# Forming and storing inner Strassen weight sums earlier in a pooling-mixer layer

## The chip, the core and the metric

The kernel runs on one core of a Trainium2 chip. Its engines are named here as the profile names them: PE is TensorE (matrix products; PEld is its weight loads), DVE is VectorE, ACT is ScalarE, POOL is GpSimd and SP is SyncE, which here only issues transfers. GpSimd issues transfers too, on a queue of its own. The metric is the device time of one execution in microseconds; lower is better. "Faster" and "slower" compare the median of the changed kernel with that of the kernel before, run on the same chip.

## The reference

One layer of a pooling mixer on 4096 tokens of width 1024, all in float32, with a residual and a final RMS norm. `rms_norm` scales a row by the inverse root of its mean square and by a weight.

```python
def pool_mixer(h, in_w, group_w, group_b, scale, out_w):
    b, s, _ = h.shape
    u, gate = jnp.split(h @ in_w, 2, axis=-1)
    ug = u.reshape(b, s, POOL_GROUPS, POOL_GROUP_DIM)
    pooled = jnp.stack([trailing_mean(ug[:, :, g], w) for g, w in enumerate(POOL_WINDOWS)],
                       axis=2) - ug
    mixed = jnp.einsum('bsgc,gcd->bsgd', pooled, group_w) + group_b
    y = mixed.reshape(b, s, POOL_WIDTH) * scale * jax.nn.silu(gate)
    return y @ out_w

# out = rms_norm(x + pool_mixer(rms_norm(x, norm_w), ...), final_norm_w)
```

There are 4 channel groups of 256 with trailing windows of 2, 4, 8 and 16 tokens. The two large products are 4096 x 1024 times 1024 x 2048 and 4096 x 1024 times 1024 x 1024.

## The kernel before, in words

**Products.** Each float32 operand is split into a high part (a copy on ScalarE, rounded to the fast matmul type) and a low part (a subtraction on VectorE). A product of two such operands is three matmuls: high by high, high by low, low by high. Every block product is cut 2 x 2 and formed by the Strassen-Winograd scheme with seven products P1 to P7 instead of eight, over sums of the operands' quarters.

**Inner products.** Some of the seven are cut 2 x 2 once more. An input P7 then takes 84 matmuls of 256 columns (`product_seven`, L741 ff., matmuls at L753) where a plain one takes 48 of 512 (`mm3`, L807). In the output phase an inner P7 or P2 takes 42 of 256 (L949) where a plain one takes 24 of 512. Inner products need sums of the weight's quarters, each split in high and low part, and sums of the operand's quarters (`split_seven` for the input, `split_inner` for the output's P2).

**Steps.** The work is a row of steps, one for each of the seven products of a block. First come 28 steps "a": four blocks of 1024 tokens against the u half of the input weight, folded with the group maps. Then 28 steps "b": the same blocks against the gate half (gate blocks 0 to 3). Then the output phase, eight blocks "o" of 512 tokens. In a and b the order is P1, P2, P7, P6, P5, P4, P3, in o it is P1, P7, P6, P2, P5, P4, P3. P7 writes the PSUM banks that P1 and P2 filled, so it starts only when ScalarE has evicted them.

**What is inner before.** In the gate half P7 of blocks 1 and 2 (`inner_in`). In the output phase P2 from block 1 and P7 from block 2 (`OWN = 2`). The weight sums for the gate half's P7 are formed by `form_seven` in gate block 0, at P7, P6, P5 and P4, and stay on chip. Those of the output phase are formed in output blocks 0 and 1 (the table `forming`, with `load_inner`, `sum_inner`, `split_weight`).

**What sets the order.** A tile scheduler places the instructions on each engine, held by `issue_after` edges; from two steps ahead of output block `OWN` the order is the written one (`InOrder`, `steady`). Each engine works through its own row of instructions in order and stops at one whose inputs or whose tile's former users aren't done. The same holds for the two queues of transfers. Working tiles come from 11 `st` and 8 `vt` slots of 512 KB; operands in split form from four `op` tiles, two for each step. `take` hands out the slot that has been free longest, `keep` takes one for good, and a later load into a reused slot waits for all that read or wrote it. Nearly every copy, sum and transfer is recorded at L79, the line of a helper, so the tile names tell them apart: `op` are split operands, `w` split weights (`w_0_77`, `w_1_78` are the halves for P1), `bank` PSUM, `inner` a slot that holds an inner weight sum, `sd` the saved operands, `t3d`, `wod`, `wvd` weights in DRAM, `yd` the gated y in DRAM.

## Time and profile before

| | |
|---|---|
| median of 3 runs | 907.3 us (906.36 to 909.16) |
| profiled execution: device time | 907.23 us |
| profiled execution: span of the records | 905.4 us |
| TensorE busy | 895.8 us, 99% |
| VectorE, ScalarE, GpSimd busy | 84%, 57%, 13% |
| granted TensorE clock | 0.998 |
| an input step, plain (48 matmuls of 512) | 10.36 us |
| an input P7 with inner products (84 of 256) | 9.60 us |
| P1 of gate block 0 starts | 324.08 us |
| P7 of gate block 0 starts | 344.80 us |
| P7 of gate block 3 starts | 561.07 us |
| output block 0 starts | 612.98 us |
| period of an output block from block 2 on | 35.28 us |

The profile's times are microseconds from the span's start. A line of a timeline has the start, the duration, the engine, the line, the operation and the tiles (written from read), and in square brackets how long the engine was idle before it and what it waited for. "x12" is a group of 12. An engine's mean duration is longer than the distance of two instructions back to back, since they overlap by about 0.09 us. The granted clock is near full throughout. The span has a further few microseconds around it that the device time counts.

### The profile page before, as it was taken

How to read it: one execution, taken by the hardware profiler on the slowest of the kernel's cores; microseconds unless marked ns; L12 is line 12 of the kernel's file. 1: busy time of each engine (PE TensorE's matmuls, PEld its weight loads, DVE VectorE, ACT ScalarE, POOL GpSimd, SP SyncE). 2: the span in 40 equal slices, each digit the busy share in tenths (PEclk: the TensorE clock that was granted, in tenths of full speed). 3: DMA queues.
4: the chain of work that ended last, by engine and by line, in shares of the span. 5: the costliest groups of instructions: out<-in, count | busy, mean ns of one | idle time of the engine just before them, and what ended most of it. 6: DMA issues, size and time to landing. Idle time of an engine off the chain costs nothing.

```text
span 905.4 us, 12216 instructions
## 1 busy us (share of the span) xinstructions
PE 895.8 (99%) x4518; PEld 791.1 (87%) x4518; DVE 757.0 (84%) x925; ACT 517.5 (57%) x853; POOL 118.5 (13%) x208
## 2 busy tenths in 40 slices
PE   9999999999999999999999999999999999999996
PEld 7888888888888888889889888888889899999995
DVE  3899995985995999797599499599798878888797
ACT  7869547547445565346545636654657466565464
POOL 0020100100110000000000000001133333343330
PEclk9999999999999999999999999999999999999999
DMA  9987767577675453333554474638483865945953
GB/s 343 401 305 226 273 239 241 187 274 233 235 267 198 164 199 103 99 112 111 202 199 135 179 279 143 197 117 239 143 236 88 212 180 147 233 153 131 259 181 116
DMA packets 71692, 180.49 MB, mean 199 GB/s; under 512 B 6608, under 2 KB 24656, under 8 KB 71632
## 3 DMA queue, kind: packets, MB, share of 16 engines
q1 hardware_dynamic: 54976, 132.50, 42.6%
q0 software_dynamic: 15936, 46.16, 17.6%
q10 hardware_dynamic: 720, 1.06, 0.3%
q8 instruction: 35, 0.57, 0.3%
q14 instruction: 25, 0.20, 0.1%
HBM read 118.86 MB, written 60.83 MB: 198 GB/s over the span
## 4 chain that ended last, share of the span: by engine, by line
PE 87%; DVE 5%; ACT 3%; DMA 2%; issue 2%; POOL 0%; SPq 0%; DVEq 0%; ACTq 0%; POOLq 0%
PE bank L807 78%; PE bank L949 5%; DVE vt L79 2%; PE bank L753 2%; DVE op L79 2%; DMA st<-yd 1%; PE bank L447 1%; DVE st L79 1%; ACT op L79 1%; DMA early<-in_wut 1%; ACT st L79 1%; ACT w L79 0%; ACT vt L79 0%; DMA st<-wod 0%; DVE w L79 0%
## 5 line engine op out<-in xcount | busy, mean ns | idle before, releaser
L807 PE MATMUL bank<-op,w 128*128 128x512 f32 x2592 | 560.9, 379 | 0.1
L807 PEld LDWEIGHTS bank<-op,w 128*128 128x128 f32 x2592 | 489.4, 189 | 70.3 <-ACT vt L79 0.5
L807 PE MATMUL bank<-w,op 128*128 128x512 f32 (+1 forms) x1044 | 230.5, 377 | 0.0
L807 PEld LDWEIGHTS bank<-w,op 128*128 128x128 f32 x1044 | 192.3, 189 | 25.0
L79 DVE TENSOR_TENSOR op<-st,op 128x1024 fp32r<-128x1024 f32 x116 | 141.0, 1222 | 49.7 <-ACT op L79 49.3
L79 ACT ACTIVATE op<-st 128x1024 fp32r<-128x1024 f32 x116 | 121.4, 1051 | 68.7 <-PE bank L807 27.6
L79 ACT ACTIVATE op<-vt 128x1024 fp32r<-128x1024 f32 x67 | 70.4, 1053 | 59.3 <-DVE vt L79 38.7
L79 ACT ACTIVATE vt<-bank 128x512 f32<-128x512 f32 (+1 forms) x124 | 69.6, 580 | 48.0 <-PE bank L807 44.2
L79 DVE TENSOR_TENSOR op<-vt,op 128x1024 fp32r<-128x1024 f32 x67 | 80.9, 1221 | 17.5 <-ACT op L79 17.4
L79 DVE TENSOR_TENSOR st<-st,st 128x1024 f32<-128x1024 f32 (+1 forms) x55 | 63.9, 1181 | 17.6 <-ACT st L79 16.8
L79 POOL DMA_DIRECT2D vt<-in_x x26 | 23.3, 937 | 390.7 <-DVE vt L79 353.8
L79 ACT ACTIVATE bank<-bank 128x512 f32<-128x512 f32 (+1 forms) x78 | 38.7, 498 | 43.5 <-PE bank L807 32.1
L79 DVE TENSOR_TENSOR vt<-bank,vt 128x512 f32<-128x512 f32 (+1 forms) x94 | 54.2, 603 | 7.1 <-PE bank L949 4.6
L79 ACT ACTIVATE st<-bank 128x512 f32<-128x512 f32 (+1 forms) x58 | 33.0, 587 | 31.2 <-PE bank L807 17.4
L79 ACT ACTIVATE st<-st 128x1024 f32<-128x1024 f32 x33 | 34.8, 1056 | 22.6 <-DVE st L79 19.6
L79 DVE TENSOR_TENSOR st<-bank,st 128x512 f32<-128x512 f32 (+1 forms) x68 | 41.2, 625 | 7.4 <-PE bank L807 4.1
L79 DVE TENSOR_TENSOR st<-st,vt 128x1024 f32<-128x1024 f32 (+1 forms) x36 | 41.6, 1175 | 2.2 <-DMA vt<-rd 2.2
L949 PEld LDWEIGHTS bank<-w,op 128*128 128x128 f32 x312 | 40.4, 191 | 1.7
L949 PE MATMUL bank<-w,op 128*128 128x256 f32 x312 | 41.1, 275 | 0.0
L79 DVE TENSOR_TENSOR w<-st,w 128x1024 fp32r<-128x1024 f32 (+1 forms) x27 | 31.6, 1182 | 9.3 <-ACT w L79 9.2
L79 DVE TENSOR_TENSOR_SCAN vt<-vt,window 128x1040 f32<-128x1040 f32 x16 | 38.0, 2381 | 0.3 <-DMA yd<-vt 0.3
L79 DVE TENSOR_TENSOR vt<-vt 128x1024 f32<-128x1024 f32 (+3 forms) x42 | 37.6, 898 | 0.1
(115 smaller groups left out, 720.7 us busy)
## 6 DMA issues: line engine op xcount, KB each, us to landing
st<-in_xt SPq DMA_DIRECT2D x28, 512.0 KB, 6.2
sd<-st POOLq DMA_DIRECT2D x28, 512.0 KB, 4.4
st<-sd SPq DMA_DIRECT2D x26, 512.0 KB, 4.5
st<-in_x SPq DMA_DIRECT2D x21, 512.0 KB, 6.3
yd<-st SPq DMA_DIRECT2D x19, 512.0 KB, 2.9
vt<-yd SPq DMA_DIRECT2D x17, 512.0 KB, 10.4
out<-vt POOLq DMA_DIRECT2D x17, 512.0 KB, 3.3
st<-wod SPq DMA_DIRECT2D x16, 512.0 KB, 4.3
```

Source lines behind the costliest of these rows:

```text
L79: r = f(*args, **kwargs)
L447: latest[0] = nc.tensor.matmul(ps, a[:, kk, 2 * j + t, :], maps, start=t + m == 0, stop=t == 1 and m == len(pairs) - 1,).ins
L753: latest[0] = nc.tensor.matmul(cell(n, c).rearrange("p (a s) -> p a s", s=2), x1, x2, start=i == P1 and k + m == 0, stop=k == 1 and m == 2 ...
L807: latest[0] = nc.tensor.matmul(ps, a, b, start=start and n == 0, stop=stop and n == 2, skip_group_check=True).ins
L949: latest[0] = nc.tensor.matmul(ps, x1, x2, start=start and k + n == 0, stop=k == 1 and n == 2, skip_group_check=True,).ins
```

## The change

There are four parts.

1. P7 of gate block 0 gets inner products too (`inner_in`, and `split_reach` for its P6, lose the condition on the block). Its weight sums are formed in the last u block: the weight halves are loaded at its P7 (`load_seven`), summed at P6 (`sum_seven`), and split and stored to DRAM at P6 and P5 (`save_seven`, into `sevend`, on GpSimd's queue). At P2 of gate block 0 `take_seven` loads them back, into a quarter of P7's weight tiles and three kept slots.
2. P7 of the output phase is inner from block 1 (`OWN = 1`). The output phase's weight sums are formed in gate blocks 2 and 3: those of P2 at P4 and P3 of block 2 and P1 of block 3, those of P7 at P2, P7, P6 and P5 of block 3. `save_inner` stores them to `innerd`, and `take_inner` loads them in output block 0, again on GpSimd's queue.
3. With the sums gone from output blocks 0 and 1, the split of P2's operand outside the steady order (`split_inner`, `late_split`) and the gathering of slots (`gathered`, `split_weight`) go.
4. In the last output block the inner sums of P2 are added before the evictions instead of behind them, the split for P4 goes behind P2's product, and one row of the norm moves from P2 to P4.

GpSimd's queue has 24 rows more, VectorE 15, ScalarE 14, TensorE 9. The diff, cut to its core:

```diff
-OWN = 2
+OWN = 1
...
-        return q == 1 and 0 < b < NB - 1 and i == P7
+        return q == 1 and b < NB - 1 and i == P7
...
+    sevend = {p: dram.tile([P, 2, 2, 256], F32R, name=f"seven{p}") for p in (P4, P5, P6, P7)}
...
+    def save_seven(*ps):
+
+        for p in ps:
+            place = next_kept()
+            t = st.keep().rearrange("p v (k c) -> p v k c", k=2)
+            latest_copy[0] = copy(t[:, 0], seven["sums"][p]).ins
+            latest_split[0] = sub(t[:, 1], seven["sums"][p], t[:, 0].bitcast(F32)).ins
+            gpsimd.dma_start(out=sevend[p], in_=t)
+            give_kept(place)
...
+    def take_seven():
...
+        for p in (P6, P7, P4):
+            places_in.append(next_kept())
+            t = st.keep().rearrange("p v (k c) -> p v k c", k=2)
+            gpsimd.dma_start(out=t, in_=sevend[p])
+            seven_w[p] = [t[:, v] for v in range(2)]
+        seven_w[P5] = [w[P7][0][:, v, :, 0:256] for v in range(2)]
+        for v in range(2):
+            gpsimd.dma_start(out=seven_w[P5][v], in_=sevend[P5][:, v])
...
-    def split_weight(i, *ps):
+    def save_inner(i, *ps):
 
         for p in ps:
+            place = next_kept()
+            t = st.keep()
+            home = versions(t)
+            latest_copy[0] = copy(home[0], raws[i][p]).ins
+            latest_split[0] = sub(home[1], raws[i][p], home[0].bitcast(F32)).ins
+            gpsimd.dma_start(out=innerd[i][p], in_=t)
+            give_kept(place)
...
+    def take_inner(i, *ps):
+        for p in ps:
+            place = innerd[i][p]
             if p == P5:
-                home = [quarter(w[i][0][:, s], 1) for s in range(2)]
+                home = [quarter(w[i][0][:, v], 1) for v in range(2)]
+                for v in range(2):
+                    gpsimd.dma_start(out=home[v], in_=versions(place)[v])
             else:
-                t = kept.pop().rearrange("p k (h s a) -> p h k s a", h=2, s=2)
-                home = [t[:, s] for s in range(2)]
-            copy(home[0], raws[i][p])
-            sub(home[1], raws[i][p], home[0].bitcast(F32))
+                t = reserved.pop() if reserved else st.keep()
+                gpsimd.dma_start(out=t, in_=place)
+                home = versions(t)
             (own_w if i == P7 else inner_w)[p] = home
...
         if inner and i == P2:
             inner["rows"] = [hs[b][0, j][:, 0] for j in range(2)]
+            if final:
+                add_inner(0, (0, 0))
...
-        if inner and i == P2:
+        if inner and i == P2 and not final:
             add_inner(0, (0, 0))
...
-            split(ready[P4], s["22"])
-            give(s.pop("22"))
-            if final:
-                norm_row(b - 1, 0, 1)
+            if not final:
+                split(ready[P4], s["22"])
+                give(s.pop("22"))
...
             evict_o(b, P2, sets)
+            if final:
+                split(ready[P4], s["22"])
+                give(s.pop("22"))
...
-            if not final:
+            if final:
+                norm_row(b - 1, 0, 1)
+            else:
...
-        (0, P4): lambda: load_inner(P2),
-        (0, P3): lambda: sum_inner(P2),
-        (1, P1): lambda: split_weight(P2, P7, P6),
-        (1, P7): lambda: (split_weight(P2, P5, P4), end_weights(P2), load_inner(P7)),
-        (1, P6): lambda: sum_inner(P7),
-        (1, P5): lambda: split_weight(P7, P7, P6),
-        (1, P4): lambda: (split_weight(P7, P5, P3), keep_temps(P7)),
+        ("a", NB - 1, P7): load_seven,
+        ("a", NB - 1, P6): lambda: (sum_seven(), save_seven(P6)),
+        ("a", NB - 1, P5): lambda: (save_seven(P7, P4, P5), end_seven()),
+        ("b", 0, P2): take_seven,
+        ("b", NB - 2, P4): lambda: load_inner(P2),
+        ("b", NB - 2, P3): lambda: (sum_inner(P2), save_inner(P2, P7, P6)),
+        ("b", NB - 1, P1): lambda: (save_inner(P2, P4, P5), end_weights(P2)),
+        ("b", NB - 1, P2): lambda: load_inner(P7),
+        ("b", NB - 1, P7): lambda: sum_inner(P7),
+        ("b", NB - 1, P6): lambda: save_inner(P7, P7, P6),
+        ("b", NB - 1, P5): lambda: (save_inner(P7, P3, P5), end_weights(P7)),
+        ("o", 0, P6): lambda: take_inner(P7, P5),
+        ("o", 0, P2): lambda: take_inner(P7, P6, P7, P3),
+        ("o", 0, P5): lambda: take_inner(P2, P5),
+        ("o", 0, P4): lambda: (reserved.extend(st.keep() for _ in range(3)), keep_temps()),
+        ("o", 0, P3): lambda: take_inner(P2, P7, P6, P4),
```

On VectorE the first place is ahead of P7 of gate block 0. Before, the row with `op_85` is the low part of P7's first operand, and the two `w` rows are the low parts of P4's weights:

```order
L79 SCALAR_TENSOR_TENSOR st_95<-vt_107,colt,st_95 128x512 x2
L79 TENSOR_TENSOR op_85<-vt_101,op_85 128x1024
L79 MEMSET vt_106 128x2x16
L79 TENSOR_REDUCE window<-vt_106 128x1
L79 TENSOR_TENSOR w_0_674<-st_94,w_0_674 128x1024
L79 TENSOR_TENSOR w_1_675<-st_99,w_1_675 128x1024
L79 TENSOR_TENSOR op_86<-st_96,op_86 128x1024
L79 TENSOR_TENSOR vt_100<-st_90,vt_101 128x1024
L79 TENSOR_TENSOR vt_104<-st_98,st_96 128x1024
```

In the changed kernel, at the same place, where `op_85` is the low part of the front sums (the second inner operand of P7 that is read) and `op_86` that of the plain quarter read first:

```order
L79 TENSOR_TENSOR w_0_686<-st_2282,w_0_686 128x1024
L79 TENSOR_TENSOR vt_104<-st_92 128x512
L79 TENSOR_TENSOR w_1_687<-st_91,w_1_687 128x1024
L79 TENSOR_TENSOR vt_104<-vt_103,vt_104 128x512
L79 TENSOR_TENSOR op_86<-st_92,op_86 128x1024
L79 TENSOR_TENSOR vt_107<-vt_104,st_92 128x512
L79 TENSOR_TENSOR vt_107<-vt_103,vt_104 128x512
L79 TENSOR_TENSOR vt_102<-st_96,st_92 128x1024
L79 TENSOR_TENSOR st_91<-st_98,vt_103 128x1024
L79 TENSOR_TENSOR op_85<-vt_107,op_85 128x1024
```

The four sums of 512 (`vt_104`, `vt_107`) are new here, and the `w` rows and the form of P6's operand (`vt_102`, `st_91`) now come ahead of the operand's low part.

The second place is ahead of P7 of gate block 3. On SyncE's queue, before, the loads for P1's weights of the output phase (`wod1`) stand ahead of the stores of y:

```order
L79 DMA st3_92<-wod1_0_123 128x1024 [waits DMAHW3_49,DVE_49]
L79 DMA st7_3691<-wod1_1_124 128x1024 [waits DVE_49]
L79 DMA yd4_173<-st2_91 128x1024 [waits DVE_49,Activation_49]
L79 DMA yd4_173<-st4_93 128x1024 [waits DMAHW6_49,DVE_49,Activation_49]
L79 DMA yd5_174<-vt1_101 128x1024 [waits DMAHW7_49,DVE_49]
L79 DMA yd5_174<-vt2_102 128x1024 [waits DMAHW0_49,DVE_49]
L79 DMA st7_3691<-wod2_0_125 128x1024 [waits DMAHW4_49,DMAHW1_49,DVE_49]
```

In the changed kernel, where a DMASW in the list of waits is a transfer of GpSimd's queue (here the store of a saved sum):

```order
L79 DMA vt7_107<-wod2_1_126 128x1024 [waits DMAHW0_49,DVE_49]
L79 DMA st10_4083<-wod1_0_123 128x1024 [waits DMAHW3_49,DMAHW1_49,DMASW3_49]
L79 DMA yd5_174<-vt3_103 128x1024 [waits DVE_49]
L79 DMA yd5_174<-vt6_106 128x1024 [waits DVE_49]
L79 DMA st9_4088<-wod1_1_124 128x1024 [waits DMAHW4_49,DMAHW6_49,DMASW4_49,Activation_49]
L79 DMA st10_4083<-wod7_1_136 128x1024 [waits DMAHW5_49,DMAHW1_49,DVE_49]
L79 DMA st2_91<-wod2_0_125 128x1024 [waits DVE_49,Activation_49]
```

The first `wod1` load moved behind a saved sum's store, the second behind both stores of block 3's y and another saved sum's store. On ScalarE the copies of those weights stood well ahead of the evictions of P2's banks (`vt_103`, `st_92`), but for the first half of P2's weights (`w_0_79`):

```order
L79 ACTIVATE w_1_78<-st_3691 128x1024
L79 ACTIVATE op_87<-st_3690 128x1024
L79 ACTIVATE w_0_79<-st_3691 128x1024
L79 ACTIVATE vt_103<-bank_69 128x512
L79 ACTIVATE vt_103<-bank_70 128x512
L79 ACTIVATE st_92<-bank_71 128x512
L79 ACTIVATE w_1_80<-st_90 128x1024
L79 ACTIVATE st_92<-bank_72 128x512
```

and now:

```order
L79 ACTIVATE w_0_77<-st_4083 128x1024
L79 ACTIVATE op_86<-st_91 128x1024
L79 ACTIVATE vt_103<-tails 128x2x16
L79 ACTIVATE w_1_78<-st_4088 128x1024
L79 ACTIVATE vt_104<-bank_69 128x512
L79 ACTIVATE vt_104<-bank_70 128x512
L79 ACTIVATE w_0_79<-st_91 128x1024
L79 ACTIVATE st_96<-bank_71 128x512
L79 ACTIVATE w_1_80<-vt_107 128x1024
L79 ACTIVATE st_96<-bank_72 128x512
```

The copy of the second half of P1's weights (`w_1_78`, from the `wod1_1` load) now stands directly ahead of the first eviction, and that of `w_0_79` between the second and the third.

116 lines of the change are left out of this document (39 added, 77 removed).

## The prediction, as recorded before the run

> **What bounds the kernel now.** I read the page first, then the chain of waits, then the busy time of each engine step by step, and last single rows at the places that the change touches. From the page, the engines' busy time and the stores that GpSimd issues:
>
> ```profile
> PE 895.8 (99%) x4518; PEld 791.1 (87%) x4518; DVE 757.0 (84%) x925; ACT 517.5 (57%) x853; POOL 118.5 (13%) x208
> ...
> sd<-st POOLq DMA_DIRECT2D x28, 512.0 KB, 4.4
> ```
>
> TensorE is the bound over the whole span, so a gain must take matmul time away, and every microsecond that another engine delivers too late is paid in full. The chain of waits (start, length, what) shows what a step costs and the few places where TensorE waits:
>
> ```profile
> 417.48 9.60 PE bank L753 x84
> 427.08 62.16 PE bank L807 x288
> 489.24 9.60 PE bank L753 x84
> ...
> 555.99 3.40 DMA st<-wod
> 559.57 0.87 issue
> 560.44 0.59 ACT vt L79
> 561.07 80.57 PE bank L807 x372
> ...
> 671.19 0.94 PE bank L949 x6
> 672.13 2.59 PE bank L807 x12
> ...
> 689.64 1.34 PE bank L949 x12
> ```
>
> Six plain input steps take 62.16 us, 10.36 each; an input P7 with inner products (L753) takes 9.60. A plain matmul of 512 columns is 2.59/12 = 0.216 us, one of 256 columns 1.34/12 = 0.112. Three stalls stand in the second half. Six matmuls at L949 should take 0.67 us; at 671.19 they take 0.94 after a wait of 0.31, so 0.58 is lost. The last block has the same, worse: 0.61 + 0.27 = 0.88. The third is where P7 of gate block 3 waits for bank evictions until 561.07 (two steps' excess in the table below: 0.22 + 0.11 = 0.33).
>
> ```profile
> 671.19 0.94 PE L949 MATMUL bank<-inner,op 128*128 128x256 f32 x6 [0.31 <-DVE vt L79]
> ...
> 885.05 0.94 PE L949 MATMUL bank<-inner,op 128*128 128x256 f32 x6 [0.61 <-DVE vt L79]
> ```
>
> The busy times by step (window, length, then each engine's busy time) show how much room stands beside TensorE. The first three rows are P7, P6, P5 of the last u block, the next two its P4 and P3, then P1, P2, P7 of gate block 0; the last three are P1, P2, P7 of gate block 3:
>
> ```profile
> core 0: us, PE busy (x) PEld busy (x) DVE busy (x) ACT busy (x) POOL busy (x), PEclk, DMA share, GB/s
> 272.28:282.64 10.36, 10.36 (x50) 9.07 (x49) 5.96 (x6) 5.35 (x7) 0.00 (x0) 1.00 0.48 163
> 282.64:293.00 10.36, 10.36 (x50) 9.07 (x49) 6.29 (x8) 6.84 (x10) 0.00 (x0) 1.00 0.68 227
> 293.00:303.36 10.36, 10.36 (x50) 9.07 (x49) 7.82 (x11) 8.72 (x11) 0.00 (x0) 1.00 0.46 162
> 303.36:313.72 10.36, 10.36 (x50) 9.07 (x49) 10.36 (x12) 2.82 (x6) 0.00 (x0) 1.00 0.64 209
> 313.72:324.08 10.36, 10.36 (x50) 9.07 (x49) 10.36 (x13) 5.82 (x7) 0.00 (x0) 1.00 0.30 115
> 324.08:334.44 10.36, 10.36 (x50) 9.07 (x49) 10.36 (x12) 6.14 (x8) 0.00 (x0) 1.00 0.74 244
> 334.44:344.80 10.36, 10.36 (x50) 9.07 (x49) 10.33 (x14) 5.34 (x7) 0.00 (x0) 1.00 0.61 201
> 540.13:550.49 10.36, 10.36 (x50) 9.07 (x49) 10.29 (x10) 4.87 (x10) 0.00 (x0) 1.00 0.26 102
> 550.49:561.07 10.58, 10.52 (x49) 8.88 (x47) 10.52 (x12) 4.70 (x7) 0.00 (x0) 1.00 0.43 154
> 561.07:571.54 10.47, 10.47 (x49) 9.18 (x49) 9.99 (x9) 7.96 (x12) 0.00 (x0) 1.00 0.48 155
> ```
>
> VectorE has 4.40 + 4.07 + 2.54 = 11.0 us free before 303.36, and none from there to 344.80, nor from 540 to 561. The change puts VectorE work into or ahead of both full stretches. That decides this case.
>
> **Gains.** P7 of gate block 0 goes from 10.36 to 9.60: 0.76. P7 of output block 1 goes from 24 matmuls of 512 (5.18) to 42 of 256 (4.69): 0.49. In output blocks 0 and 1, sixteen VectorE rows that sum and split weights go away, and the steady order begins where VectorE is freer: I take the 0.58 as gone. Reading the inner sums first in the last block frees the first bank before the evictions: I take the 0.88 as gone too; the pieces moved behind (a split, a norm row) have the P5 to P3 products to hide under. Together 2.71. The earlier sums of output weights (gate blocks 2 and 3) cost TensorE nothing themselves; their price is at the second place below. The 24 new transfers on GpSimd's queue: 12 stores, 12 loads and the split loads; GpSimd is 13% busy and its loads for P7 of gate block 0 are issued where the front of the queue is free, so I cost their issue at nothing, and their landing below.
>
> **The first place: P7 of gate block 0.** Durations on VectorE, with spacing (back to back, a pair's length less one row's):
>
> ```profile
> 336.69 0.76 DVE L79 SCALAR_TENSOR_TENSOR st<-st,colt,st 128x512 f32<-128x512 f32 x1
> 337.36 1.42 DVE L79 SCALAR_TENSOR_TENSOR st<-vt,colt,st 128x512 f32<-128x512 f32 x2
> 338.68 1.23 DVE L79 TENSOR_TENSOR op<-vt,op 128x1024 fp32r<-128x1024 f32 x1
> ...
> 340.06 2.35 DVE L79 TENSOR_TENSOR w<-st,w 128x1024 fp32r<-128x1024 f32 x2
> ```
>
> So 1.13 for a row of 1024, 0.66 for a scaled row of 512; a plain row of 512 is 0.69 long (next fence), 0.60 spaced. Before, the operand of P7 is ready at 339.91, 4.9 us ahead of 344.80. Now ahead of it stand four weight sums, four low parts for the saves, four sums of the operand (4.8 + 2.4 us in rows of 512) and two rows of the P6 form and two of w4 (4.5 us, which stood behind): 11.7 us. The chain begins with loads that VectorE waits for at 291.90 and 295.85. SyncE's issues, then VectorE's rows, then the group of plain rows of 512:
>
> ```profile
> 286.85 0.38 SPq L79 DMA_DIRECT2D vt<-in_in_w  x1
> ...
> 290.42 0.34 SPq L79 DMA_DIRECT2D st<-t3d  x1
> ```
>
> ```profile
> 291.90 1.41 DVE L79 SCALAR_TENSOR_TENSOR vt<-vt,colt,st 128x512 f32<-128x512 f32 x2 [1.51 <-DMA vt<-in_in_w]
> ...
> 295.85 1.41 DVE L79 SCALAR_TENSOR_TENSOR st<-st,colt,st 128x512 f32<-128x512 f32 x2 [2.54 <-DMA st<-t3d]
> ```
>
> ```profile
> L79 DVE TENSOR_TENSOR inner<-vt,inner 128x512 fp32r<-128x512 f32 x4 | 2.7, 688 | 0.0
> ```
>
> Issue to use is 5.05 and 5.43. In the new order the load waits for two scaled rows fewer and is issued 1.3 us sooner, so the scaled rows start at 290.6. From there to the low part of the fourth saved sum stand 6 scaled rows, 5 of 1024 and 9 of 512: 4.0 + 5.7 + 5.4 = 15.1, ending at 305.7. Its store lands 4.4 later (310.1); only then may SyncE load the second t3 half into that slot, and 5.3 later (315.4) VectorE can scale with it. By its own work (6 more rows of 1024, 3 of 512: 8.6) it would be there at 314.3. Behind that load on SyncE stand the in_in_w loads for w4 and two y stores; none is wanted before VectorE has passed the scaling. From 315.4 to the low part of the front sums, P7's second inner operand, stand 14 scaled rows, 19 of 1024 and 6 of 512: 9.2 + 21.5 + 3.6 = 34.3, ending 349.7. TensorE wants it six short matmuls into the step, at 345.5: 4.2 late. ScalarE's three copies ahead of the inner moves (about 1.05 each) hold the next bank some 0.6 longer. So P7 is 4.8 late and 0.76 shorter: +4.0. Bounds: if VectorE comes to 303 with all the added rows done in its 11.0 us, nothing is late (-0.8); if landings are a third slower, as the busy DMA rows of 0.64 and 0.74 allow, 1.5 and 1.8 more (+7.3). I stay in the middle because the rows name each wait.
>
> [...]
>
> **The second place: P7 of gate block 3.** Here the weights w1 of the output phase must be copied by ScalarE before it may evict P2's banks, which P7 needs:
>
> ```profile
> 559.47 1.06 ACT L79 ACTIVATE w<-st 128x1024 fp32r<-128x1024 f32 x1 [5.88 <-DMA st<-wod]
> 560.44 1.07 ACT L79 ACTIVATE vt<-bank 128x512 f32<-128x512 f32 x2
> ...
> 552.59 0.32 SPq L79 DMA_DIRECT2D yd<-vt  x1
> 555.99 6.15 SPq L79 DMA_DIRECT2D st<-wod  x4
> ```
>
> Before, only the w2 copy stands ahead of the evictions, issued at 555.99 and used at 559.47 (3.48). Now the second w1 half does, and its load waits on SyncE behind both stores of y, and for the store of the last saved P2 sum to land. VectorE has eight rows of 512 more before the y rows (4.8 us): the last y store goes from 552.59 to 557.3, the last saved sum, 3.4 us of rows ahead, ends at 553.9, its store lands at 558.3, the load is issued then and used at 561.8. Copy (1.05) and eviction (0.6) end at 563.4 instead of 561.0: 2.6 late on a step that would start at 550.49 + 10.36 = 560.85. The third bank stands behind the w2 copy: its load follows a VectorE row four of 1024 behind the y rows (561.8), arrives 565.3, copy and eviction end at 566.9, where TensorE wants the bank at 563.4 + 2.6 = 566.0: 0.9 more. In all 3.5 in place of 0.33: +3.2. Bounds: nothing late (-0.3), or with landings as long as at the first place, twice 1.7 more (+6.6).
>
> **The sum.** The profiled run took 907.23 with a span of 905.4; the median of the runs is 907.3, so the sum is taken on 907.2. 907.2 + 4.0 + 3.2 - 0.49 - 0.58 - 0.88 = 912.5 us, 0.6% slower.
>
> **The rivals.** Other side: VectorE comes early. Its busy rows before 344 need not mean that it is behind: with 11.0 us idle before 303 it could run the moved rows there, and at gate block 3 likewise in the steps ahead of 518. It decides from 4.2 us earlier at the first place and 2.6 at the second. Against it: the sums hang on loads that land at 290.6 at the earliest. Then 907.2 - 0.76 - 0.33 - 1.95 = 904.2. Only the first place stalls: 907.2 + 4.0 - 0.33 - 1.95 = 908.9. Only the second: 907.2 - 0.76 + 3.2 - 1.95 = 907.7. Worse than forecast: a third place, where GpSimd's loads of the saved sums in output block 0 stand ahead of the x loads on its queue, and wait for VectorE's w3; a store and a load there (4.4) on top, 916.9. Against it: VectorE is freer there by sixteen rows. That the change would not do what it says is ruled out by the order of its instructions.
>
> **How the numbers follow.** Both places 0.56, VectorE early 0.16, only the first 0.09, only the second 0.06, worse 0.13. What a measurement can tell from no change is about 0.3%, 2.7 us: 904.6 to 910.0. Faster is the early case, 0.16. Same is the two single cases (0.15) and a tenth of the first, 0.21 in all. Slower is the rest, 0.63. The likeliest case alone spans 909.5 to 916. The range goes from 904.0, which takes in the early case, to 917.5, for the third place or the longer landings at one place.
>
> **What would show it.** In the new profile: the L753 group of 84 from about 345 ending near 359.2, with a wait for VectorE's op; a gap of about 2.6 before P7 of gate block 3 behind ScalarE's w1 copy from wod, and one of about 0.9 inside it; no wait of L949 for VectorE at the start of the steady order or in the last block. I am wrong if the operand's low part stands ready before 345.5, if ScalarE's w1 copy there ends by 560, or if TensorE waits at the first output blocks.

## The result and the profile after

The changed kernel takes 934.53 us (median of 5 runs, 933.53 to 935.35) against 907.3 us: the ratio is 1.0297, with a 95% interval from 1.0282 to 1.0313. The forecast was 912.5. The direction was right and the size was not: 27.2 us slower in place of 5.2. The profiled execution took 933.88 us with a span of 932.1. From the page, the engines' busy time:

```profile
PE 902.8 (97%) x4572; PEld 797.9 (86%) x4572; DVE 766.1 (82%) x939; ACT 523.1 (56%) x868; POOL 136.0 (15%) x235
```

TensorE has 54 matmuls more (the nine rows of the change are groups of six) and was "busy" 7 us longer, though the inner products should have taken 1.25 us of work away. A part of the time is therefore inside the matmuls, and the rest is waits. The loss of a step is the distance from its first matmul to that of the next step, less 10.36 us (9.60 for an inner P7 of the input). Laid out by place, in us:

| place | before | after |
|---|---|---|
| P6 and P5 of u block 2 | 0.10 | 0.77 |
| P1, P2, P7 of gate block 0 | none | 0.65, 3.78, 5.42 |
| P2 of gate block 1 | none | 1.21 |
| P2, P7 of gate block 3 | 0.23, 0.10 | 4.67, 1.91 |
| output block 1, whole period | 36.35 | 45.60 |
| from the last matmul to the end of the span | 7.0 | 8.1 |

Against the profile before, gate block 0 costs 9.85 of loss less the 0.76 that its inner P7 saves, +9.1; gate block 1 +1.2; gate block 3 +6.25; output block 1 +9.25; u block 2 +0.7 (the run with repeated low parts, below, changes nothing there and has 0.73 as well, so this isn't put down to the change); the tail +1.1. The stall in the last output block is gone, -0.9. The sum is +26.7, the difference of the spans. Three places carry it.

**The first place, P7 of gate block 0.** TensorE's timeline; the idle time before a group and what it waited for stand in the brackets:

```profile
349.89 0.94 PE L761 MATMUL bank<-op,w 128*128 128x256 f32 x6 [3.62 <-ACT vt L79]
351.69 0.58 PE L761 MATMUL bank<-op,w 128*128 128x256 f32 x1 [0.86 <-ACT op L79]
354.00 4.00 PE L761 MATMUL bank<-op,w 128*128 128x256 f32 x17 [1.74 <-DVE op L79]
```

The step begins with a wait of 3.62 us for an eviction on ScalarE, then waits for the high and the low part of its operand. And 17 matmuls of 256 columns take 4.00 us, 0.235 each, where 0.112 is usual. ScalarE's and VectorE's timelines show what was late:

```profile
307.32 0.63 ACT L79 ACTIVATE inner<-vt 128x512 fp32r<-128x512 f32 x1 [2.90 <-DMA seven<-inner]
...
348.30 1.06 ACT L79 ACTIVATE op<-vt 128x1024 fp32r<-128x1024 f32 x1 [2.48 <-DVE vt L79]
349.26 0.58 ACT L79 ACTIVATE vt<-bank 128x512 f32<-128x512 f32 x1
```

```profile
307.98 0.69 DVE L79 TENSOR_TENSOR inner<-vt,inner 128x512 fp32r<-128x512 f32 x1 [3.32 <-ACT inner L79]
...
319.38 1.41 DVE L79 SCALAR_TENSOR_TENSOR st<-st,colt,st 128x512 f32<-128x512 f32 x2 [2.09 <-issue]
...
347.51 0.69 DVE L79 TENSOR_TENSOR vt<-vt,vt 128x512 f32<-128x512 f32 x1
...
352.72 2.36 DVE L79 TENSOR_TENSOR op<-vt,op 128x1024 fp32r<-128x1024 f32 x2
```

ScalarE's copy of the front sums (348.30) waits for VectorE's second sum (347.51), and the eviction that P7's first matmul needs stands right behind that copy. VectorE works without a break from 319.38. Its first wait (307.98) is for ScalarE's copy of the fourth saved sum, which itself waited for the store of an earlier one to land (307.32). Its second wait is put down to "issue", but it ends 0.1 us behind the landing (319.29) of a load that SyncE issued at 312.41, 7.0 us before its use:

```profile
312.41 0.32 SPq L79 DMA_DIRECT2D st<-t3d  x1
```

**The second place, P7 of gate block 3.** From the chain of waits:

```profile
564.92 4.38 DMA inner<-inner
...
569.35 5.53 DMA st<-wod
...
574.92 0.94 issue
575.86 0.59 ACT vt L79
...
576.49 63.58 PE bank L815 x285
```

The store of a saved sum lands after 4.38 us, the load of `wod1_1` waits for it, lands 5.53 later, ScalarE copies it (0.94 to the next instruction), evicts, and TensorE starts.

**The third place, P7 of output block 1.** TensorE, then ScalarE's square root that holds up the move of the bank, then GpSimd's queue:

```profile
680.70 1.65 PE L957 MATMUL bank<-w,op 128*128 128x256 f32 x6 [7.56 <-ACT bank L79]
682.14 1.49 PE L957 MATMUL bank<-inner,op 128*128 128x256 f32 x6
683.42 2.67 PE L815 MATMUL bank<-w,op 128*128 128x512 f32 x6
```

```profile
676.41 0.29 ACT L79 ACTIVATE otmp<-oss,eps 128x2 f32<-128x2 f32 x1 [5.56 <-POOL oss L79]
```

```profile
645.24 0.91 POOL L79 DMA_DIRECT2D w<-inner  x1 [1.45 <-issue]
653.24 0.89 POOL L79 DMA_DIRECT2D w<-inner  x1 [7.08 <-issue]
...
666.84 0.91 POOL L79 DMA_DIRECT2D w<-inner  x1 [5.15 <-PE bank L815]
670.85 0.90 POOL L79 DMA_DIRECT2D w<-inner  x1 [3.10 <-issue]
...
676.15 0.23 POOL L79 TENSOR_TENSOR oss<-parts 128x2 f32<-128x2 f32 x1
```

GpSimd forms the sum of squares for the norm at 676.15. Ahead of it in its queue stand the loads of P5's saved sums (`w<-inner`, two for each sum, in pieces of 128 float32). The second of a pair is issued 8.0 and 4.0 us behind the first, and the wait before it has no releaser ("issue"). The second pair itself starts late, behind a wait of 5.15 us for TensorE.

### The profile page after: what moved, and what is told of

It reads as the page before. It is cut to its first block, busy times and chain, and to the rows that moved or that the text cites. A ratio compares the mean times of both kernels' runs of the same rounds, so it can differ in the third digit from the quotient of the medians.

```text
span 932.1 us, 12430 instructions
## 1 busy us (share of the span) xinstructions
PE 902.8 (97%) x4572; PEld 797.9 (86%) x4572; DVE 766.1 (82%) x939; ACT 523.1 (56%) x868; POOL 136.0 (15%) x235
## 4 chain that ended last, share of the span: by engine, by line
PE 43%; DVE 11%; issue 5%; DMA 5%; ACT 1%; POOL 1%; DVEq 0%; POOLq 0%; ACTq 0%; SPq 0%
PE bank L815 34%; PE bank L957 5%; DVE vt L79 5%; PE bank L761 3%; DVE st L79 3%; DVE op L79 2%; DMA vt<-yd 1%; DMA out<-vt 1%; ACT st L79 1%; DMA st<-wod 1%; DMA vt<-in_x 1%; DMA inner<-inner 0%; DVE w L79 0%; DMA st<-t3d 0%; DMA seven<-inner 0%
## 5 line engine op out<-in xcount | busy, mean ns | idle before, releaser
L815 PE MATMUL bank<-op,w 128*128 128x512 f32 x2544 | 553.2, 380 | 6.3 <-ACT vt L79 4.5
L815 PEld LDWEIGHTS bank<-op,w 128*128 128x128 f32 x2544 | 481.2, 189 | 76.8 <-ACT vt L79 4.9
L815 PE MATMUL bank<-w,op 128*128 128x512 f32 (+1 forms) x1020 | 227.2, 378 | 0.0
L79 DVE TENSOR_TENSOR op<-st,op 128x1024 fp32r<-128x1024 f32 x121 | 147.3, 1222 | 54.2 <-ACT op L79 53.8
L79 ACT ACTIVATE op<-st 128x1024 fp32r<-128x1024 f32 x121 | 126.9, 1052 | 73.5 <-PE bank L815 33.9
L957 PE MATMUL bank<-w,op 128*128 128x256 f32 x336 | 45.1, 278 | 7.6 <-ACT bank L79 7.6
L79 POOL DMA_DIRECT2D inner<-inner x14 | 7.7, 548 | 291.3 <-DVE inner L79 255.6
L79 ACT ACTIVATE st<-bank 128x512 f32<-128x512 f32 x56 | 32.2, 594 | 31.3 <-PE bank L815 19.1
L79 ACT ACTIVATE w<-st 128x1024 fp32r<-128x1024 f32 (+1 forms) x24 | 24.6, 1035 | 34.1 <-DMA st<-wod 21.5
L79 DVE TENSOR_TENSOR vt<-vt 128x256 f32<-128x256 f32 (+3 forms) x44 | 38.4, 876 | 0.1
```

Of the source, the lines that this page charges most:

```text
L79: r = f(*args, **kwargs)
L815: latest[0] = nc.tensor.matmul(ps, a, b, start=start and n == 0, stop=stop and n == 2, skip_group_check=True).ins
L957: latest[0] = nc.tensor.matmul(ps, x1, x2, start=start and k + n == 0, stop=k == 1 and n == 2, skip_group_check=True,).ins
```

## The experiments

All ratios are against the kernel before on the same chip, with their 95% intervals. The losses are read as in the table above, from the profiled execution, which isn't always near the median: it took 929.12 us in the first run on GpSimd's queue, 923.88 in the run without part 1 and 911.50 in the first of the two runs with a plain P7.

### The parts alone

The first run holds part 4 alone, in the kernel before (the diff of `norm_row`, `split` and `add_inner` shown above, and nothing else).

> The kernel before with the change's fourth part alone: in the last output block the inner sums of P2 are read ahead of the evictions, the split for P4 and a norm row are moved behind. Theory: the 0.88 us that TensorE loses in the last block before goes and nothing takes its place, 906.4 us, a ratio of 0.999. Rival: the end of the span is bound by the last norm rows and stores, and the moved norm row makes that tail longer (in the changed kernel 8.1 us lie between the last matmul and the end, before 7.0): no gain, 907.3 to 907.6.

It took 906.84 us, 0.9996 (0.9987 to 1.0005). The wait of 0.61 us is gone, but TensorE's last block isn't shorter for it: 36.43 us from its first matmul to the end of its last, 36.41 before. The last matmul ends at 897.39 in place of 898.40 because the block started 1.0 us earlier, and 0.9 of that stood there already at P1 of gate block 0, which part 4 doesn't touch. Another wait stands in the block now, at its P7:

```profile
867.96 0.94 PE L949 MATMUL bank<-w,op 128*128 128x256 f32 x6 [0.32 <-ACT bank L79]
```

From the last matmul to the end of the span it is 8.3 us in place of 7.0. This tail is 7.0 to 7.1 us in the traces of all kernels without part 4 and 7.3 to 8.4 in all with it. In the changed kernel TensorE's last block does get shorter, 35.53 us, and the longer tail takes it back. Which of the moved pieces lengthens it was not tried. No difference in the time can be measured.

The second holds part 1 alone: the saved sums and the inner P7 of gate block 0.

> The kernel before with the change's first part alone: inner products in P7 of gate block 0, its weight sums formed in the last u block, stored and loaded. Theory: the whole loss between 324 and 365 us of the changed kernel is this part's own, since a saved sum waits for an earlier store out of its slot and the t3 load for the last store: P6 of gate block 0 starts some 9 us later than before, 916 to 917 us. Rival: the part as such costs what the prediction summed (4 us), and the rest of the loss there comes with the other parts' transfers and the changed order: 911 to 912 us.

It took 917.58 us, 1.0119 (1.0105 to 1.0133). P1, P2 and P7 of gate block 0 lose 1.31, 3.77 and 5.13, P2 of gate block 1 loses 1.20, and the rest is as before. The first place is a matter of part 1 alone, and nothing later catches up with it.

The third is the changed kernel without part 1, so that the inner P7 begins in gate block 1 again:

```diff
-        return q == 1 and b < NB - 1 and i == P7
+        return q == 1 and 0 < b < NB - 1 and i == P7
...
-    def sum_seven():
+    def form_seven(stage):
```

> The changed kernel without its first part (P7 of gate block 0 plain, the gate half's weight sums formed in gate block 0 as before). Theory: the losses at the three places are independent and add up: 934.5 less the 10.2 us of e2, 924 to 925 us, with the waits ahead of P7 of gate block 3 (6.3 us over before) and at P7 of output block 1 (10.3) unchanged. Rival: the second and third place inherit their lateness from the first: 912 to 918 us.

It took 927.17 us, 1.0231 (1.0201 to 1.0260), with runs from 923.88 to 931.14. That is 7.4 us below the changed kernel where part 1 alone costs 10.2, so the parts add up only roughly. Gate block 3 loses 6.24 and 1.87 and output block 1 takes 46.06. The second and the third place come without the first.

### The third place: GpSimd's queue

In the changed kernel only the issuer of the loads of P5's saved sums is changed:

```diff
-                    gpsimd.dma_start(out=home[v], in_=versions(place)[v])
+                    sync.dma_start(out=home[v].bitcast(F32), in_=versions(place)[v].bitcast(F32))
```

> The changed kernel with the loads of the two P5 sums into quarters of weight tiles (128x4x128, pieces of 512 bytes, in output block 0) on SyncE's queue instead of GpSimd's; nothing else changed. Theory: in the changed kernel the second quarter load of each pair waits 4 to 8 us for room in GpSimd's queue, behind it stand the x loads, the other inner loads and the small sum that ScalarE's evictions of output block 1 wait for; without them P7 of output block 1 loses its 7.7 us wait and the slow matmuls behind it, 924 to 925 us. Rival: the transfers between 640 and 680 are bound by the DMA engines' share of 0.9 and more, on whichever queue they stand: within 2 us of 934.5.

It took 925.5 us, 1.0196 (1.0178 to 1.0213), 0.5 above what the theory expected. TensorE at the same place:

```profile
678.21 0.94 PE L957 MATMUL bank<-w,op 128*128 128x256 f32 x6 [0.48 <-ACT bank L79]
```

The wait is 0.48 us in place of 7.56, and output block 1 takes 36.03. So four loads on a queue make the third place. The other way to show it is to give GpSimd's transfers more scratch space (`dynamic_dma_scratch_size`; that a transfer waits for room in it is the author's reading, the traces show only when the loads go out):

```diff
-        "TRN2", target_bir_lowering=False, num_devices=1, dynamic_dma_scratch_size=1024
+        "TRN2", target_bir_lowering=False, num_devices=1, dynamic_dma_scratch_size=1536
```

> The changed kernel with the scratch space for GpSimd's transfer descriptors at 1536 bytes instead of 1024; nothing else changed. Theory of room in the queue: the waits of GpSimd without a releaser (11.6 us for the quarter loads of weights) get shorter by a third or more, and the wait of 7.6 us ahead of P7's inner matmuls in output block 1 with them, 926 to 932 us. Rival (the DMA engines' bandwidth, or VectorE): the waits and the time stay, 934 to 935 us.

It took 934.2 us, 1.0298 (1.0284 to 1.0312), no different from the changed kernel. The stall in output block 1 is nevertheless gone: it takes 35.62. The first pair of loads is now issued 1.6 us apart, and in exchange TensorE waits in later blocks, for the longest in blocks 2 and 7:

```profile
643.31 1.19 POOL L79 DMA_DIRECT2D w<-inner  x1
644.92 0.89 POOL L79 DMA_DIRECT2D w<-inner  x1 [0.42 <-issue]
```

```profile
711.75 0.94 PE L957 MATMUL bank<-w,op 128*128 128x256 f32 x6 [2.16 <-ACT bank L79]
...
893.86 1.06 PE L957 MATMUL bank<-w,op 128*128 128x256 f32 x6 [2.36 <-ACT bank L79]
```

Blocks 2 to 6 take 37.71, 35.61, 36.11, 36.54 and 35.94 in place of 35.28. Whether the larger scratch space itself does that was tried in the kernel before, with the same one-line edit:

> The kernel before with the scratch space for GpSimd's descriptors at 1536 bytes instead of 1024; nothing else changed. In e4 that took away the 10 us wait in output block 1 and the later blocks' P7 lost as much. Theory: the larger space lets GpSimd issue the x loads in a bunch, which hurts the later output blocks by itself: 912 to 917 us here. Rival: it needs the changed kernel's order (P7 inner from block 1, other slots): 907 to 908 us.

It took 911.66 us, 1.0047 (1.0032 to 1.0062). Blocks 3 to 6 take 35.40, 35.94, 35.91 and 36.69, and TensorE's waits stand in the same form:

```profile
835.49 0.94 PE L949 MATMUL bank<-w,op 128*128 128x256 f32 x6 [1.14 <-ACT bank L79]
872.51 0.94 PE L949 MATMUL bank<-w,op 128*128 128x256 f32 x6 [1.47 <-ACT bank L79]
```

So with 1536 the second load of the first pair goes out sooner, 1.6 us behind the first in place of 8.0 (the second pair stays 4.2 us apart), and 1536 costs the steady blocks by itself. Why it does was not settled.

### The first place: forming, loading, or the block's own inner P7

A first theory was that too few slots are free. The fifth sum is split straight into its place in the weight tile, without a slot, a store and a load:

```diff
+    def split_five():
+        home = [w[P7][0][:, v, :, 0:256] for v in range(2)]
+        latest_copy[0] = copy(home[0], seven["sums"][P5]).ins
+        latest_split[0] = sub(home[1], seven["sums"][P5], home[0].bitcast(F32)).ins
...
-        ("a", NB - 1, P5): lambda: (save_seven(P7, P4, P5), end_seven()),
+        ("a", NB - 1, P5): lambda: save_seven(P7, P4),
+        ("a", NB - 1, P4): lambda: (split_five(), end_seven()),
```

> The first part alone (as in e2), but P5's weight sum is split straight into its quarter of P7's weight tile one step later, not stored and loaded; the other three sums go through DRAM as before. Theory: in e2 the fourth save waits 3.3 us for the second save's store out of the same slot, and the next t3 load for the fourth store and its own landing; without the fourth save that load starts when the second store has landed, VectorE comes some 4 us sooner to the front sums, and the time is 913 to 914 us instead of 917.6. Rival: VectorE's rows or the full DMA engines around 310 us set it, not the slot: within 1 us of 917.6.

It took 919.13 us, 1.0128 (1.0113 to 1.0144): no gain. P2 loses 10.01 now and P7 1.60. The whole delay stands in one wait for the eviction ahead of P7:

```profile
355.65 4.44 PE L764 MATMUL bank<-op,w 128*128 128x256 f32 x24 [9.85 <-ACT st L79]
```

VectorE could scale the `t3d` halves from 312.98 on, 5.8 us sooner than in the run of part 1 (318.78), which fits that the slot of the save held that load. But the edit also reordered ScalarE's row: the copy ahead of the eviction waits 4.90 us for a sum from VectorE, and P7 starts 6.4 us later than there. One slot and one store less are not enough.

Next, part 1 alone without VectorE's eight rows that form the weight sums and their low parts (ScalarE copies the unsummed halves in their place; the sums and the low parts of these weights are left out of the computation):

> As e2 (the first part alone) with VectorE's eight rows for the gate half's weight sums left out: the quarters take the place of the sums, and ScalarE writes the low parts as copies; slots, stores and loads stay. Theory of VectorE's work: its stretch from 305 to 354 us has 8 rows of 0.60 less ahead of it, P7 of gate block 0 is up to 4.8 us less late, 912.5 to 914.5 us against 917.6. Rival (slots and landings of the stores): the saved slots come free as late as before, 917 to 918 us.

It took 916.37 us, 1.0093 (1.0078 to 1.0108), 1.2 us below part 1 alone, or 2.4 by the ratios, since the runs of the kernel before beside it were 0.65 us slower. VectorE's work is smaller by eight rows of 512 columns, 4.8 us at the spacing used in the prediction, and P7 starts 1.4 us earlier (347.89 for 349.28). Its timeline shows why, and TensorE's has the same shape as before:

```profile
316.21 1.42 DVE L79 SCALAR_TENSOR_TENSOR st<-st,colt,st 128x512 f32<-128x512 f32 x2 [3.94 <-DMA st<-t3d]
```

```profile
347.89 0.94 PE L757 MATMUL bank<-op,w 128*128 128x256 f32 x6 [1.16 <-ACT vt L79]
...
352.00 4.00 PE L757 MATMUL bank<-op,w 128*128 128x256 f32 x17 [1.74 <-DVE op L79]
```

VectorE waits 3.94 us for the second `t3d` load, which is there 2.6 us sooner than in the run of part 1. The chain hangs on when that load arrives; most of what is saved in the rows ahead of it goes into the wait.

The next two runs hold the forming, storing and loading of part 1, but P7 of gate block 0 stays plain. In the first the loads stand three steps later:

```diff
-        return q == 1 and b < NB - 1 and i == P7
+        return q == 1 and 0 < b < NB - 1 and i == P7
...
-        ("b", 0, P2): take_seven
+        ("b", 0, P5): take_seven
```

> Part 1 without the use that pays for it: the four weight sums are formed, split and stored in the last u block and loaded back as in the changed kernel, but P7 of gate block 0 stays plain (48 matmuls of 512), so its operand needs no sums, and the loads are issued three steps later, where nothing waits for them. If forming and storing in the last u block is what makes P7 of gate block 0 late (the sums of the fourth save wait for a store out of their slot and for the second t3 half, and VectorE is behind by that much), P7's operand still comes about 3 us late, since of VectorE's new rows ahead of it only 2.4 us of operand sums and 4.5 us of moved rows go: about 910 to 911.5. If block 0's own inner P7 makes the delay (operand sums, rows that its split pulls ahead, three loads into kept slots), nothing is late and the time is that before plus some noise: 907 to 908.5.

It took 908.79 us, 1.0018 (1.0007 to 1.0029), with runs from 907.57 to 911.5. In the second the three loads into slots stand at P2 of gate block 0 again, and only the fourth, into the weight tile that plain P7 uses, stays later:

```diff
-        ("b", 0, P5): take_seven
+        ("b", 0, P2): take_seven,
+        ("b", 0, P5): take_fifth
```

> Part 1's forming, storing and loading with P7 of gate block 0 plain, as in e13_form_only (908.8 us), but with three of the four saved sums loaded back at P2 of gate block 0 as in the changed kernel, into three slots that are kept from there on. If the slots and loads are what makes block 0's inner P7 late, the delay comes back without the inner P7: 913 to 917. If it is the operand's rows and the bank moves of the inner P7 itself, the time stays at 908 to 909.5.

It took 909.25 us, 1.0023 (1.0014 to 1.0033). VectorE waits in both as it does in the changed kernel; the rows are those of the second run, the waits for ScalarE's copy and for the `t3d` load:

```profile
308.22 0.69 DVE L79 TENSOR_TENSOR inner<-vt,inner 128x512 fp32r<-128x512 f32 x1 [4.43 <-ACT inner L79]
...
319.00 1.41 DVE L79 SCALAR_TENSOR_TENSOR st<-st,colt,st 128x512 f32<-128x512 f32 x2 [1.48 <-issue]
```

So the late load is there and costs 1.5 to 2.0 us by itself by the medians; 8.2 to 8.8 of part 1's 10.2 appear only when gate block 0 uses the sums. The cost of the load varies with its landing: in the profiled execution of the first run, the slowest of its ten, VectorE has it at 320.93, and P1 of gate block 0 loses 4.84 behind a wait of 2.89 for VectorE; in that of the second VectorE has it at 319.00, and P1 loses 1.14. A plain P7 needs VectorE's low part of one operand and an eviction that waits for no sum. The inner P7 needs VectorE's four sums and the rows pulled ahead with them first, and ScalarE's evictions stand behind copies of those sums. The two together are late; forming and loading alone is not late by much. The use alone can't be run, since it needs the sums, so how the 8.2 to 8.8 divide between rows and evictions is argued from these rows, not shown.

### The second place: slots and landings

In the changed kernel without part 1, the slots of the last two saved P2 sums are given back two steps later, so that the `wod1` loads go elsewhere:

```diff
-            give_kept(place)
+            if i == P2 and p in (P4, P5):
+                late_places.append(place)
+            else:
+                give_kept(place)
...
-        ("b", NB - 1, P7): lambda: sum_inner(P7),
+        ("b", NB - 1, P7): lambda: (give_kept(*late_places), sum_inner(P7)),
```

> As e6, but the two slots out of which the last two sums of P2 are stored in gate block 3 are given back at P7, so that the w1 loads go into other slots and wait for no store of a sum. Theory: the wait ahead of P7 of gate block 3 comes from these slots; it falls from 4 to 6 us to under 1, and the time from e6's 924 or so to 918 to 920 us. Rival: VectorE's full stretch (the y rows and the stores of y ahead of the loads on SyncE) holds P7 anyway: within 2 us of e6.

It took 920.57 us, 1.0141 (1.0123 to 1.0160). The total is 0.6 us above what was expected, but not for the reason: gate block 3 still loses 7.49. No copy of the `wod1` weights waits for its load any more, but on ScalarE the copy into a saved sum's slot now waits 7.52 us (3.16 without the edit) for a store of y out of that slot, ahead of the moves of the banks:

```profile
555.06 0.63 ACT L79 ACTIVATE inner<-st 128x512 fp32r<-128x512 f32 x1 [7.52 <-DMA yd<-st]
```

The gain came from output block 1 (42.75 in place of 46.06). One slot was freed and the next one waited.

Then the sums of P2 are left out (what is stored for them is copied unsummed from DRAM to DRAM on GpSimd's queue, so P2's inner products are not the reference's):

```diff
-        ("b", NB - 2, P4): lambda: load_inner(P2),
-        ("b", NB - 2, P3): lambda: (sum_inner(P2), save_inner(P2, P7, P6)),
-        ("b", NB - 1, P1): lambda: (save_inner(P2, P4, P5), end_weights(P2)),
...
+        ("b", NB - 1, P6): lambda: (plain_inner(P2), save_inner(P7, P7, P6)),
```

> As e6 (the change without its first part), but P2's inner weight sums of the output phase are not formed: no loads, sums, splits and slots for them in gate blocks 2 and 3; four plain quarters of the weight are copied from DRAM to DRAM in their place, so this kernel leaves out the sums themselves. Theory: all of the 8 us lost around P7 of gate block 3 comes from P2's sums, and goes: 918 to 920 us against 927 for e6, the wait in output block 1 unchanged. Rival: the sums of P7 or the order of the w loads hold gate block 3: 925 us or more.

It took 925.31 us, 1.0189 (1.0172 to 1.0206). Gate block 3 loses less, 2.87 and 0.20, but P2 of gate block 2 now loses 4.41 and the first two output blocks take 37.05 and 47.04. The edit moved other work as well, and the run is inconclusive on what the sums cost.

Leaving out only VectorE's eight rows for P2's sums, with loads, copies and stores in place (sums and low parts of P2's saved weights are left out of the computation):

> As e6 with VectorE's eight rows for P2's output weight sums left out in the same way (quarters for the sums, the low parts as copies by ScalarE); slots, loads and stores stay. Theory of VectorE's work: P7 of gate block 3 is up to 4.8 us less late, 921 to 923 us against 927. Rival (slots): the copy that holds ScalarE ahead of the evictions waits for a transfer out of its slot, not for VectorE, 925 to 928 us.

It took 927.25 us, 1.0213 (1.0198 to 1.0229), the same as with those rows (927.17). P2 of gate block 3 loses 8.87, and output blocks 0 and 1 take 41.23 and 43.38, so this edit moved other work too. Fewer rows on VectorE bring no gain that can be measured here; that VectorE plays no part isn't shown.

Last, the sums of P2 are formed in output block 0, where the kernel before formed them, and stay on chip; those of P7 stay in gate block 3:

```diff
-        ("b", NB - 2, P4): lambda: load_inner(P2),
-        ("b", NB - 2, P3): lambda: (sum_inner(P2), save_inner(P2, P7, P6)),
-        ("b", NB - 1, P1): lambda: (save_inner(P2, P4, P5), end_weights(P2)),
...
-        ("o", 0, P2): lambda: take_inner(P7, P6, P7, P3),
-        ("o", 0, P5): lambda: take_inner(P2, P5),
+        ("o", 0, P2): lambda: (take_inner(P7, P6, P7, P3), load_inner(P2)),
+        ("o", 0, P5): lambda: sum_inner(P2),
```

> As e6, but P2's output weight sums are formed in output block 0, from the load to the split, without DRAM; P7's are still formed in gate block 3 and stored. Theory: gate block 3 loses nothing (8 us less), GpSimd's queue has half the pieces of 512 bytes in output block 0 and the wait in output block 1 shrinks from 10 us to under 5: 909 to 914 us, at best below the kernel before. Rival: VectorE, full in output block 0, is late with the operands of output block 1 by the eight rows it gets back: 915 to 920 us.

It took 917.95 us, 1.0110 (1.0092 to 1.0128). The wait at P7 of gate block 3 is nearly gone:

```profile
554.54 45.64 PE L807 MATMUL bank<-op,w 128*128 128x512 f32 x209 [0.66 <-ACT bank L79]
```

Gate block 3 loses 0.93 and 0.26, and the second place is therefore due to forming and saving P2's sums there. Output block 0 takes 40.17 now in place of 36.26, so over half of what is won comes back there; block 1 takes 40.38 in place of 46.06. With P5's loads on SyncE's queue as well (the edit of the third place):

> The kernel of the run before with P2's sums formed in output block 0 and P7's in gate block 3 (918.0 us), with the two quarter loads of P7's saved sum put on SyncE's queue instead of GpSimd's. Its output blocks 0 and 1 took 40.17 and 40.38 us in place of 36.3. If GpSimd's queue, which its two quarter loads hold up, is what stalls P7 of output block 1, block 1 falls to about 36 and the time to 913 to 914.5; block 0 keeps its excess. If the stalls of both blocks come from VectorE's and ScalarE's rows of the P2 sums, the time stays at 916 to 918.5.

It took 912.77 us, 1.0056 (1.0039 to 1.0072). Output block 1 takes 36.05, block 0 takes 42.29: GpSimd's queue held block 1 here too, and what P2's sums cost in block 0 stays. None of these versions is measurably faster than the kernel before.

### The slow matmuls behind a wait

Behind each of the three waits matmuls ran at about half their rate: 0.235 us each for 256 columns at the first place (0.112 is usual), 0.43 for 512 at the second (0.216), 1.49 us for six of 256 at the third (0.83). The granted clock of the changed kernel was halved in these three stretches, from the windows view (window, length, then busy time and count by engine, PEclk, DMA share, GB/s):

```profile
351.36:358.19 6.83, 4.77 (x20) 4.47 (x21) 6.83 (x7) 5.24 (x10) 0.00 (x0) 0.50 0.03 9
576.64:580.05 3.41, 3.41 (x9) 2.69 (x10) 3.34 (x4) 1.19 (x2) 0.00 (x0) 0.50 0.45 154
675.62:685.87 10.25, 5.17 (x18) 4.72 (x19) 7.90 (x11) 7.10 (x17) 6.23 (x12) 0.50 0.47 149
```

Behind the wait of 7.56 us the clock is at 0.50 when the first matmul starts, behind that of 4.51 from 0.15 us later on; behind that of 3.62 six matmuls ran at full rate first. The "some 4 us" of the two expectations below lies between 3.62 and 4.51, and their 3.4 and 1.7 us are what the second place shows: eight matmuls, 0.43 us apart in place of 0.216. To see whether the wait itself does this, one VectorE row of the kernel before was repeated in output blocks 2 to 6. The first attempt repeated a row of `split_o`:

```diff
-            sub(s["3"], s["11"], s["21"])
+            for _ in range({2: 6, 3: 9, 4: 12, 5: 16, 6: 21}.get(b, 1)):
+                sub(s["3"], s["11"], s["21"])
```

> The kernel before with one VectorE row (the difference for P7's operand, 128x1024) repeated 6, 9, 12, 16 and 21 times in output blocks 2 to 6, so that TensorE waits once in each block, longer from block to block; the result stays the same. If a wait beyond some 4 us halves TensorE's rate for a while behind it, the matmuls of 512 behind the short waits stand 0.216 us apart and those behind the long ones 0.43 us, for about 3.4 us, so each long wait costs up to 1.7 us more than its own length. If the slow matmuls of the changed kernel came from something else (weights or operands that arrive late one by one), the matmuls behind these waits run at 0.216 whatever the wait's length.

These blocks don't run that function (the written order has its own code), the instructions stayed those of the kernel before, and the run (906.64 us) says nothing. The second attempt repeats a row of the written order:

```diff
-            low(sums_op, v)
+            for _ in range({2: 4, 3: 7, 4: 10, 5: 13, 6: 18}.get(b, 1)):
+                low(sums_op, v)
```

> The same test as in the run before (e14_stalls), in the written order this time: the low part of the inner sums' operand (VectorE, 128x1024) is written 4, 7, 10, 13 and 18 times over in output blocks 2 to 6, so that TensorE waits for it, longer from block to block; the result stays the same. If a wait beyond some 4 us halves TensorE's rate behind it, matmuls of 256 columns there stand 0.22 us apart in place of 0.112 and those of 512 columns 0.43 in place of 0.216, for about 3.4 us, and a long wait costs up to 1.7 us more than its length, a short one only its length. If the slow matmuls had another cause, they run at full rate behind each of these waits.

Of the matmuls of 256 columns, TensorE's timeline shows the first groups behind waits of 0.74, 3.84, 7.62 and 17.39 us:

```profile
729.75 0.94 PE L949 MATMUL bank<-w,op 128*128 128x256 f32 x6 [0.74 <-ACT bank L79]
730.52 0.83 PE L949 MATMUL bank<-inner,op 128*128 128x256 f32 x6
...
744.62 1.22 PE L949 MATMUL bank<-w,op 128*128 128x256 f32 x4 [3.84 <-DVE op L79]
745.63 1.49 PE L949 MATMUL bank<-inner,op 128*128 128x256 f32 x6
...
790.49 1.22 PE L949 MATMUL bank<-w,op 128*128 128x256 f32 x4 [7.62 <-DVE op L79]
791.51 1.49 PE L949 MATMUL bank<-inner,op 128*128 128x256 f32 x6
...
895.20 1.22 PE L949 MATMUL bank<-w,op 128*128 128x256 f32 x4 [17.39 <-DVE op L79]
896.21 1.49 PE L949 MATMUL bank<-inner,op 128*128 128x256 f32 x6
```

Behind 0.74 us the second group of six takes 0.83, as long as such a group usually takes; behind 3.84, 7.62 and 17.39 it takes 1.49. The starts of single matmuls lie 0.214 us apart there (0.427 for 512 columns), and the granted clock is full again 5.1, 3.6 and 4.7 us behind the first matmul (5.9 behind the wait of 11.40 in block 5). The wait makes them slow, and a longer wait doesn't make them slow for longer.

Shorter waits can do it too, as the granted clock in the traces shows. In the changed kernel the ends of the three stretches above, from 351.36 to 685.87, lie 6.83, 218.45, 3.41, 95.57 and 10.25 us apart, which is 2, 64, 1, 28 and 3 times 3.41. Cut into stretches of 3.41 us at these marks, the three at whose end the clock was halved hold 2.47, 3.26 and 2.49 us in which TensorE was idle (from 347.95, 573.23 and 672.21). The one from 344.53, with 1.68 us, was followed by the full clock, and no other at the full clock between 150 us and the last matmul has more than 1.25. Two other runs have stretches with idle times between these. The first line below is one with 2.06 us idle (3.41 less the 1.35 busy), from the run without VectorE's rows for P2's sums; it lies in a wait of 2.26 us, and the stretch behind it, the second line, ran at 0.50. The last line has 1.97 us idle, from the run with P2's sums in output block 0; a wait of 2.40 us fell across two stretches there, and the clock stayed full:

```profile
654.32:657.73 3.41, 1.35 (x7) 0.84 (x5) 0.55 (x1) 0.00 (x0) 2.12 (x3) 1.00 1.11 305
657.73:661.14 3.41, 3.21 (x8) 2.58 (x9) 3.38 (x6) 0.88 (x1) 0.53 (x1) 0.50 1.12 205
...
646.13:649.54 3.41, 1.44 (x7) 1.31 (x8) 2.42 (x4) 2.10 (x4) 0.88 (x1) 1.00 1.06 316
```

## Why the prediction was right or wrong

**Gains.** The matmul time went as worked out for the two inner P7. The stall of 0.88 us in the last block is gone in the changed kernel, but the step "the pieces moved behind have the P5 to P3 products to hide under" failed for the end of the span, which came 1.1 us later behind the last matmul. The run of part 4 alone shows no gain either: there other waits took the place of the stall, and the end came 1.3 us later. The 0.58 of the first steady block wasn't won: even with GpSimd's queue cleared a wait of 0.48 stands there, and as made, 7.56.

**First place: right mechanism, sum too small (+4.0 forecast, +9.1 measured, and +1.2 more in gate block 1, a wait for a bank on ScalarE that the prediction had no term for).** From the load to the low part of the front sums, VectorE took 34.6 us (319.38 to 353.95) where 34.3 were worked out. The failed terms are these. The load was to be usable at 315.4, which is 316.1 in this execution, whose gate block 0 began 0.7 later; it was usable at 319.38. Of the 3.3 us, 1.7 is the landing (7.0 for the assumed 5.3). The rest stands ahead of its issue: the fourth saved sum needs a slot out of which the second one's store had not landed, and VectorE waited 3.32 for ScalarE's copy behind it. The prediction followed the slot of the load and missed the slot of the save. Then the "0.6" for ScalarE's copies: the eviction that P7 needs stands behind a copy that itself waits for VectorE's sums, so P7 began 3.6 us late, before a single operand was asked for. And 2.1 us are slow matmuls, for which the prediction had no term. The forecast's bound, +7.3, was too low as well.

The transfers of 512 KB took different times from issue to landing or use: the store of the fourth saved sum, at 309.08, 3.3 us, the store and the load at the second place 4.4 and 5.5, and the second `t3d` load 7.0.

**Second place: the chain as forecast, its prices too low (+3.2 forecast, +6.25 measured, inside the stated +6.6).** The store of the last saved sum landed 4.4 us after its issue, and the load was issued at once, then ScalarE's copy and the eviction followed, as predicted. The failed term is the load's landing, 5.53 for 3.48; TensorE's wait was 4.51 for 2.6. The third bank wasn't late by itself (the forecast gave it 0.9). 1.7 us more are slow matmuls: eight of 512 columns lay 0.43 apart instead of 0.216. That the sum lies inside the bound is luck, since the bound was made of two longer landings and the runs show one, and the slow matmuls. Moving P2's sums away removed the place, so what it hangs on is shown; that VectorE's extra rows make it late is not, since leaving eight of them out brought no measurable gain.

**The third place was given 0.13 and 4.4 us; it cost 9.25.** The failed step is "I cost their issue at nothing" for GpSimd's transfers. The argument was GpSimd's low busy share. What counted was how long its queue stood still, and that isn't busy time: it waited 7.1 and 3.1 us ahead of the second loads, and the sum of squares for the norm stood behind them, ScalarE's square root behind that, the move of the bank behind that. The rival that got 0.13 named the queue, but with another wait (for VectorE's w3) and under half the price. "VectorE is freer there" was no argument against it, as the long waits shown ahead of the sum of squares have no releaser or are for TensorE. The sign that the prediction gave for itself, a wait of TensorE at the first output blocks, is this one. Two changes of that queue alone, another issuer and more scratch space, took the stall away.

**The rivals.** VectorE coming early is excluded: at the first place the operand's low part was there at 353.95, about 8 us behind the 345.5 that a gain needed (346.2 in this execution). Both single cases are excluded as well, since the first and the second place each lost time. The sum that follows from the profile is 907.2 + 9.1 + 1.2 + 6.25 + 9.25 - 0.9 + 0.7 + 1.1 = 933.9, the time of the profiled execution. Of the 21.4 us by which that is above the forecast, the third place makes 10.3 (9.25 lost where 0.49 and 0.58 were to be won), the first 5.1 and the 1.2 behind it, the second 3.05, the tail 1.1, and 0.7 isn't the change's.

**What stays open.** Why the larger scratch space makes the steady blocks wait; what makes output block 0 take 40 to 42 us with P2's sums formed there; how the first place's cost divides between VectorE's rows and ScalarE's evictions; and whether the traffic of the saved sums is what makes that landing 7.0 us long, which the DMA share at the end of this document suggests and no run tried.
